# Two mixture-of-experts layers: the rows of the expert weights laid out by neighbours on a partition

## The chip, the cores and the metric

The kernel runs on one core of a Trainium2 chip, as one program. The metric is the device time of an execution in microseconds. The core has five engines that this text names as the profile does: PE (TensorE, products), whose loads of the stationary operand are shown as PEld, DVE (VectorE), ACT (ScalarE), POOL (GpSimd) and SP (SyncE), which issues most of the DMA.

## The reference

It is a block of two layers over 512 tokens of 1024 channels, in float32. The first layer is a convolution and dilated attention, a cross attention over 256 memory rows, and a mixture of experts. The second has a state space branch, a forgetting attention, and a mixture of experts of its own. The change touches the two mixtures only. For each token a router takes the best of 4 groups and in it the best 2 of 8 experts; the expert computes

```python
def expert_block(args):
    xb, e = args
    return (jax.nn.silu(xb @ w1[e]) * (xb @ w3[e])) @ w2[e]
```

and the outputs are summed with the gates of the two experts. The first layer's experts have w1 and w3 of [1024, 512] and w2 of [512, 1024], 6.29 MB each; the second layer's (there w_expert_gate, w_expert_up, w_expert_down) are half as wide, 256, and 3.15 MB. Both have 32.

## The kernel before

**Experts.** Every expert gets 64 slots; two experts make a pair of 128 slots, so there are 16 pairs per layer (`experts`, L1188). Tokens beyond the slots go in further units (`rest`, and for the second layer one unit within the stream). A pair runs through `up`, `down` and `scatter`. `up` (L1075) multiplies xg, the gathered token columns in 8 K chunks of 128 channels, by the up weights; the weights are the moving operand of 512 columns, and each expert's 64 slots are a stationary operand of 64 columns, so the two experts' products run side by side on PE's two halves. An fp32 product is two records in the profile. SiLU and the product of the two branches give hg. `down` (L1093) transposes hg in chunks of 128 (L1098), copies them to hgT, and multiplies by w_down in two halves of 512 output columns (L1110). `scatter` (L1115) multiplies by a one-hot matrix in fp32r (L1125, L1126) and DVE adds to the residual stream X (L1128).

**Gather.** In the first layer `gather` (L1059) makes xg for two pairs at a time by products: the stationary operand is a chunk of 128 channels of the token rows (hh and hl, high and low part, L1066 and L1067), the moving one the one-hot matrix. The gain of the norm is put on per channel while the result is copied out of PSUM. In the second layer the rows come from DRAM by an indirect DMA (`fetch`) and `columns` (L1147) transposes them; `first_columns` makes the first 128 slots by products.

**Weights.** `loads` (L1000) makes the list of loads of a pair: tiles of 1 MB (8 KB on a partition). In the first layer a pair has 12: two halves of the K rows for w1 and for w3 (L1027), and two halves of the output columns for w_down (L1016), of each expert. In the second layer a pair has 6: two K halves, each with gate and up side by side (two DMAs, L1027), and one w_down (L1020), per expert. SyncE issues them in this order into a ring of buffers; before the layer begins 16 or 17 are on their way (`ahead`, `step`). In DRAM a K chunk is 128 rows that follow each other, row p to partition p:

```python
return w[e, rows, cols].rearrange("(c p) n -> p c n", p=128)
```

so what one partition takes in one run is a row, or half of one: 2 KB in the first layer, 1 KB (gate, up) and 4 KB (w_down) in the second.

**Order.** The program is written as a sequence, but the order on each engine is made by the framework's planner, which simulates the program on a timeline of its own (`schedule_with_timeline_sim=True`). So products of the next pair's up stand between those of this pair's scatter.

Of the kernel before, what the change touches and what calls it, by code (L numbers as in the profile page):

```python
# [33 lines left out]
class Halves:  # L34
    """Weight tiles out of a pool of 16 KB tiles."""
# [11 lines left out]
class Slots:  # L47
    """The next 8 KB of a ring of weights; the ring may run over several pools."""
# [10 lines left out]
class K:  # L59
# [58 lines left out]
    def split(self, pool, pieces, eng=None):  # L118
        """float32 [128, kc, n] pieces into high and low parts of 12 bits each, by K chunk."""
# [15 lines left out]
    def load_unit(self, cols, kc=8):  # L135
        """256 columns of a [kc * 128, n] weight (in pieces)"""
        t = self.wt().rearrange("p (c n) -> p c n", c=8)
        o = 0
        for c in cols:
            w = c.shape[1]  # L140
            self.nc.sync.dma_start(t[:, :kc, o:o + w], c.rearrange("(c p) n -> p c n", p=128))
            o += w
        return t[:, :kc, :o]
# [7 lines left out]
    def heads_T(self, wk, tpt, r4, qT, kh, kl, i):  # L151
        """Rows r4 [128, 2 blocks, (2 q, 2 k), 64] transposed, per head: (high; low) of q, (high; high) and
        (low; low) of k on the partitions, so that two products make q k exactly."""
# [18 lines left out]
    def tok_mm(self, act, ws, tiles, nb, n, first=True, last=True, kcs=None):  # L172
        """tiles[b // per] accumulate act^T @ w for token blocks; several blocks share a bank"""
# [10 lines left out]
    def col_mm(self, act, ws, tiles, nt, width, act_c0=0):  # L184
        """tiles accumulate w^T @ act: weight columns on the partitions"""
# [19 lines left out]
    def rsq(self, pool, out, src, scale, eps):  # L205
        """out = (src * scale + eps) ** -0.5 on small tiles, by Newton's iteration."""
# [14 lines left out]
    def raw_T(self, psum, xb, gcol, hi, lo, nb, tag="tp", tpb=2):  # L221
        """x, transposed, times the gain, in two parts"""
# [16 lines left out]
    def norm_T(self, work, psum, xb, gcol, hi, lo, nb, tpb=2):  # L239
        """x (scaled in place by 1/rms), transposed, times the gain, in two parts"""  # L240
# [20 lines left out]
def red2pi(nc, pool, x, shape, name, rounds, shift=0.0):  # L261
    """x (may be modified) -> reduced to [-pi, pi], in place."""
# [18 lines left out]
def load_cols(k, a, rows, ps):  # L281
    """Every per-channel vector as columns: cols[:, i] holds 128 channels."""
# [21 lines left out]
def clamp_sin(nc, pool, out, r, shape, shift, name):  # L304
    """sin(r + shift) for r in about [-pi, pi]."""
# [33 lines left out]
def count_mask(k, wm, lnm, W, row, rep):  # L339
    """8 ln(number of branches that hold the key), or -1e30, as a function of q - k: made once for the  # L340
    1023 distances, then laid out along the diagonals by way of DRAM."""
# [26 lines left out]
def dense1(k, a, Xt, m1, ring1, more, dram, dbg):  # L368
# [7 lines left out]
    # before the residual stream is in it, its tile holds what the first phase needs in float32  # L376
# [7 lines left out]
    with ExitStack() as st:  # L384
# [15 lines left out]
        # ---- norms of x and mem  # L400
        hT = k.pair(k.big_l)
        with ExitStack() as s0:
# [22 lines left out]
            # the rows go in as they are, 1/rms onto the products  # L425
# [11 lines left out]
            # ---- convolution branch, channels on partitions  # L437
# [17 lines left out]
        with ExitStack() as s0:  # L455
# [64 lines left out]
            def after(n, what):  # L520
                """Keep the tensor engine's part of it behind the n-th last product of scores."""
                with tc.issue_after(marks[-n]):
                    what()
# [110 lines left out]
            # 1/rms of the attention output goes onto the product  # L634
# [5 lines left out]
        # ---- output projection, cross attention  # L640
# [39 lines left out]
        def xq(h):  # L680
            # keys and values of the head
# [76 lines left out]
class Moe:  # L758
    """Two-level routing, then every expert over 64 slots of its tokens.

    Tokens beyond that go in units of 128: one of them in the stream of experts where `spare` is set,
    the others in a loop. The norm's 1/rms is not on the gathered rows but on the products.
    Rows are gathered by products with one-hot matrices; or, with `rows`, from a copy in DRAM that holds
    a token's row, its gates and 1/rms."""
# [4 lines left out]
    def __init__(self, k, X, ff, w_a, w_b, w_down, gname, wg, bg, wr, br, spare, rows=None):  # L769
        self.rows = rows  # L770
        self.k, self.X, self.ff, self.spare, self.tag = k, X, ff, spare, gname
        self.w_a, self.w_b, self.w_down = w_a, w_b, w_down
        self.wg, self.bg, self.wr, self.br = wg, bg, wr, br

    def consts(self, pool):
        k, nc = self.k, self.k.nc
        self.gcol = k.gcol(self.tag, 8)
        self.brow = pool.tile([128, 36], F32, name="brow" + self.tag)
# [11 lines left out]
    def snapshot(self, pool):  # L790
        """Where the rows go that the experts gather."""
        self.hh, self.hl = [t.rearrange("p a b -> p (a b)").rearrange("p (b d) -> p b d", b=NB) for t in self.k.pair(pool)]

    def feed(self, wk, tp, pl, u):
        """256 columns of the finished residual stream: rows in two parts, squares, router."""
# [21 lines left out]
    def route(self, keep, wn, st):  # L817
        """Norm, router, ranks: keep gets what the experts need."""
# [22 lines left out]
        def warm(x, n):  # L841
            """keeps the clock of the tensor engine up while it has nothing to do"""
# [12 lines left out]
        def argmax(vals, n, m, name):  # L855
            """the first place of the max over the last axis, as a one-hot row"""
# [11 lines left out]
        # the best two experts of every group, the best group  # L868
# [14 lines left out]
        # e * 64 + 1  # L883
# [13 lines left out]
        # slot + 1, or 0  # L897
# [6 lines left out]
        # the first slots' one-hot matrix  # L904
# [12 lines left out]
    def gates(self, wn, t, gl, gm, gs, m4, As, e1, r, cnt):  # L917
        """What the scatter needs: softmax over the groups, and over the two experts; the units of the
        tokens beyond the slots."""
# [19 lines left out]
        # okey: e * 512 + rank  # L939
# [23 lines left out]
        # how the tokens beyond the slots are cut into units  # L963
# [19 lines left out]
    # ---- experts  # L983
# [6 lines left out]
    def weights(self, es, wt, q=None):  # L990
        """Weights of the experts (indices, or one dynamic slice): K chunks by expert."""
# [8 lines left out]
    def loads(self, es, W, wt, q=None):  # L1000
        """What loads a tile each, in the order of their use."""
# [4 lines left out]
        def src(w, e, rows, cols=slice(None)):  # L1006
            if isinstance(e, int):
                return w[e, rows, cols].rearrange("(c p) n -> p c n", p=128)
            return w[e, rows, cols].rearrange("a (c p) n -> p (a c) n", p=128)

        def load_down(dst, e, h):
            """w_down, by halves of its columns"""
            t = wt()
            if self.ff == 512:
                t = t.rearrange("p (c n) -> p c n", c=4)
                q.dma_start(t, src(self.w_down, e, slice(0, 512), slice(h * 512, h * 512 + 512)))  # L1016
                dst[4 * h:4 * h + 4] = [t[:, j] for j in range(4)]
            else:
                t = t.rearrange("p (c n) -> p c n", c=2)
                q.dma_start(t, src(self.w_down, e, slice(0, 256)))  # L1020
                dst[:] = [t[:, j, i * 512:i * 512 + 512] for i in range(2) for j in range(2)]

        def load(ws, dst, e, h, c=4):
            t = wt().rearrange("p (c n) -> p c n", c=c)
            n = t.shape[2] // len(ws)
            for i, w in enumerate(ws):
                q.dma_start(t[:, :, i * n:i * n + n], src(w, e, slice(h * c * 128, (h + 1) * c * 128)))  # L1027
            dst[h * c:h * c + c] = [t[:, j] for j in range(c)]
# [11 lines left out]
    def ahead(self, wt, n, order=()):  # L1040
        """n tiles may be under way before their use, in this order of their use's places."""
# [11 lines left out]
    def pair(self, p):  # L1053
        """Weights of a pair, all of its loads emitted."""
        while any(x is None for part in self.early[p] for e in part for x in e):
            self.todo.pop(0)()
        return self.early[p]

    def gather(self, wk, ps, sel, n, first=False):  # L1059
        nc = self.k.nc  # L1060
        xg = wk.tile([128, KC, 256], F32, name="xg", bufs=1)
        for c in range(KC):
            p = (self.idle_bank(ps, c) if first else ps.tile([128, 512], F32, name="g"))[:, :n]
            for b in range(NB):
                cs = slice(c * 128, (c + 1) * 128)
                nc.tensor.matmul(p, self.hh[:, b, cs], sel[:, b, :n], start=b == 0, stop=False)  # L1066
                nc.tensor.matmul(p, self.hl[:, b, cs], sel[:, b, :n], start=False, stop=b == NB - 1)  # L1067
            g = self.gcol[:, c:c + 1]
# [6 lines left out]
    def up(self, wk, ps, xg, W, parts, r, own=None):  # L1075
        """parts: (expert of W, slot range in xg, partition range out)"""
# [16 lines left out]
    def down(self, wk, ps, hg, W, parts):  # L1093
# [3 lines left out]
        for j in range(nt):  # L1097
            nc.tensor.transpose(pt[:, j * 128:(j + 1) * 128], hg[:, j * 128:(j + 1) * 128], k.ident)  # L1098
# [1059 lines left out]
```

## Time and profile before

| What | Value |
| --- | --- |
| Median of 3 runs | 1862.99 us (1860.67 to 1866.47) |
| Span of the profiled execution | 1851.7 us |
| Its own device time | not on the page; the median is 11.3 us above the span |
| PE busy | 1742.1 us, 94% of the span |
| DVE, ACT, POOL busy | 945.8, 557.4, 326.2 us |
| Granted PE clock, mean | 0.982 |
| DMA | 397.61 MB, mean 215 GB/s |

The span reaches from the first to the last instruction of one execution. A share of busy time is an average over stages; the first layer's experts run from about 508 to 1085 us, the second layer's from about 1530 us to the end. Starts and lengths of PE's instructions overlap, since products are pipelined; what a product costs is seen from the distance of the starts.

### The profile page before, as it was taken

How to read it: one execution, taken by the hardware profiler on the slowest of the kernel's cores; microseconds unless marked ns; L12 is line 12 of the kernel's file. 1: busy time of each engine (PE TensorE's matmuls, PEld its weight loads, DVE VectorE, ACT ScalarE, POOL GpSimd, SP SyncE). 2: the span in 40 equal slices, each digit the busy share in tenths (PEclk: the TensorE clock that was granted, in tenths of full speed). 3: DMA queues.
4: the chain of work that ended last, by engine and by line, in shares of the span. 5: the costliest groups of instructions: out<-in, count | busy, mean ns of one | idle time of the engine just before them, and what ended most of it. 6: DMA issues, size and time to landing. Idle time of an engine off the chain costs nothing. (4 is left out here: it accounts for less than half of the span.)

```text
span 1851.7 us, 26034 instructions
## 1 busy us (share of the span) xinstructions
PE 1742.1 (94%) x10153; PEld 1163.3 (63%) x10153; DVE 945.8 (51%) x2104; ACT 557.4 (30%) x1192; POOL 326.2 (18%) x435
## 2 busy tenths in 40 slices
PE   7999999999899999999999987999999999999998
PEld 5999999989744444434343345788997883334433
DVE  8984566554626333343333357714664554464454
ACT  5365666443212111000001033333656322112111
POOL 2211121112202210311123013201222401010000
PEclk9999999999899999999999998989999999999999
DMA  6322232326588999999899872624441957999991
GB/s 186 98 80 62 76 115 85 108 70 228 132 286 305 389 355 333 377 345 351 316 347 349 311 203 35 106 66 91 69 69 43 333 171 242 369 371 369 370 330 47
DMA packets 265873, 397.61 MB, mean 215 GB/s; under 512 B 15003, under 2 KB 147282, under 8 KB 265745
## 3 DMA queue, kind: packets, MB, share of 16 engines
q1 hardware_dynamic: 248648, 369.15, 60.5%
q0 software_dynamic: 5680, 16.75, 3.1%
q10 hardware_dynamic: 11416, 9.99, 1.8%
q8 instruction: 82, 1.34, 0.3%
q14 instruction: 47, 0.38, 0.1%
HBM read 386.87 MB, written 9.51 MB: 214 GB/s over the span
## 5 line engine op out<-in xcount | busy, mean ns | idle before, releaser
L1128 DVE TENSOR_TENSOR X<-X,y 128x512 f32<-128x512 f32 x264 | 173.6, 684 | 216.0 <-PE y L1126 215.2
L114 PE MATMUL mm<-wh,b 128*128 128x256 f32 x832 | 235.0, 285 | 3.1 <-DVE rb L510 1.6
L115 PE MATMUL mm<-wl,b 128*128 128x256 f32 x832 | 235.7, 284 | 2.3 <-POOL wl L128 2.1
L116 PE MATMUL mm<-wh,b 128*128 128x256 f32 x832 | 233.8, 284 | 0.0
L1086 PE MATMUL h<-w,xg 128*64 128x512 f32 x712 | 200.7, 599 | 0.0
L128 POOL TENSOR_TENSOR wl<-w,wh 128x1024 fp32r<-128x1024 f32 x38 | 92.8, 2443 | 496.6 <-ACT wh L125 430.3
L125 ACT ACTIVATE wh<-w 128x1024 fp32r<-128x1024 f32 x112 | 118.4, 1058 | 144.5 <-PE mm L115 68.6
L115 PEld LDWEIGHTS mm<-wl,b 128*128 128x128 f32 x832 | 158.4, 190 | 4.2 <-POOL wl L128 2.5
L114 PEld LDWEIGHTS mm<-wh,b 128*128 128x128 f32 x832 | 157.7, 190 | 5.0 <-issue 1.9
L116 PEld LDWEIGHTS mm<-wh,b 128*128 128x128 f32 x832 | 157.9, 191 | 0.5
L1120 ACT ACTIVATE oh<-o,gate 128x512 fp32r<-128x512 f32 x64 | 44.0, 688 | 317.0 <-PE o L1110 243.5
L114 PE MATMUL mm<-b,wh 128*128 128x512 f32 x320 | 125.3, 404 | 5.6 <-ACT wh L125 2.5
L115 PE MATMUL mm<-b,wh 128*128 128x512 f32 x320 | 128.0, 400 | 1.3 <-DVE b L203 1.3
L116 PE MATMUL mm<-b,wl 128*128 128x512 f32 x320 | 125.5, 397 | 0.3 <-DVE wl L128 0.3
L1125 PE MATMUL y<-oh,sT 128*128 128x512 f32 x256 | 115.2, 463 | 11.2 <-DVE X L1128 7.9
L1110 PE MATMUL o<-w,hgT 128*64 128x512 f32 (+1 forms) x384 | 117.0, 609 | 6.7 <-DVE hgT L1102 5.8
L128 DVE TENSOR_TENSOR wl<-w,wh 128x1024 fp32r<-128x1024 f32 x74 | 95.0, 1284 | 46.0 <-ACT wh L125 45.6
L1110 PE MATMUL o<-b,hgT 128*64 128x512 f32 x392 | 113.9, 608 | 3.7 <-DVE hgT L1102 3.2
L1125 PEld LDWEIGHTS y<-oh,sT 128*128 128x128 f32 x256 | 46.4, 187 | 111.6 <-issue 45.7
L1086 PEld LDWEIGHTS h<-w,xg 128*64 128x64 f32 x712 | 56.7, 136 | 89.3 <-issue 85.5
L1086 PE MATMUL h<-b,xg 128*64 128x512 f32 x312 | 101.6, 601 | 0.0
L1126 PE MATMUL y<-ol,sT 128*128 128x512 f32 x256 | 98.4, 398 | 0.4 <-DVE ol L1121 0.2
(679 smaller groups left out, 3244.2 us busy)
## 6 DMA issues: line engine op xcount, KB each, us to landing
w<-in_w_dram SPq DMA_DIRECT2D x124, 1024.0 KB, 10.2
b<-in_w_dram SPq DMA_DIRECT2D x68, 1024.0 KB, 9.6
b<-in_w_expert_down_dram SPq DMA_DIRECT2D x20, 1024.0 KB, 10.1
w<-in_w_expert_gate_dram SPq DMA_DIRECT2D x36, 512.0 KB, 9.7
w<-in_w_expert_up_dram SPq DMA_DIRECT2D x36, 512.0 KB, 9.0
w<-in_w_in_dram SPq DMA_DIRECT2D x17, 1024.0 KB, 11.5
b<-in_w_expert_gate_dram SPq DMA_DIRECT2D x30, 512.0 KB, 10.1
b<-in_w_expert_up_dram SPq DMA_DIRECT2D x30, 512.0 KB, 10.2
```

Of the source, the lines that this page charges most:

```text
L114: nc.tensor.matmul(out, sh, mh, start=start, stop=False, skip_group_check=True)
L115: nc.tensor.matmul(out, sh, ml, start=False, stop=False, skip_group_check=True)
L116: nc.tensor.matmul(out, sl, mh, start=False, stop=stop, skip_group_check=True)
L125: nc.scalar.activation(hi[:, :kc, :n], src, AF.Copy)
L128: e.tensor_sub(lo[:, :kc, :n], src, f(hi[:, :kc, :n]))
L1086: nc.tensor.matmul(h[po], xg[:, c, ss], fw[e][c], start=c == 0, stop=c == KC - 1, skip_group_check=True)
L1110: nc.tensor.matmul(o[po], hT[:, j, po], W[2][e][half * nt + j], start=j == 0, stop=j == nt - 1, skip_group_check=True)
L1120: self.k.last = nc.scalar.activation(oh, outs[half], AF.Copy, scale=gate)
L1125: nc.tensor.matmul(y, sT[:, bs], oh, start=True, stop=False)
L1126: nc.tensor.matmul(y, sT[:, bs], ol, start=False, stop=True)
L1128: nc.vector.tensor_add(xs, xs, y)
```

## The change

A run of neighbouring rows goes to one partition: with c rows per partition, partition p takes rows p*c to p*c + c - 1, which lie side by side in DRAM. For w1 and w3 c is 4 (of each half of the K rows), so a run has 8 KB in the first layer and 4 KB in the second. K chunk c of a half then holds every fourth channel, and xg must have its channels in the same order: the gather, `columns` and `first_columns` take their stationary operand with a step of 4 elements (`chan`), and the gains are loaded again in that order (`gain`, one more small DMA per layer on GpSimd's queue). w_down is cut by rows in both layers, 256 rows to a tile with c = 2, runs of 8 KB; the transposes of hg take every second column. In the first layer a tile of w_down now serves both halves of the outputs for two of four K chunks. The second layer's up weights lie as all of gate's chunks and then all of up's, so the moving operand of a product is two runs of 256. The calls in `whole` pass the gain vectors on. Comments of the file are taken out too.

```diff
 class Moe:
-    def __init__(self, k, X, ff, w_a, w_b, w_down, gname, wg, bg, wr, br, spare, rows=None):
+    def __init__(self, k, X, ff, w_a, w_b, w_down, gname, gain, wg, bg, wr, br, spare, rows=None):
...
+        self.g = gain
...
     def consts(self, pool):
...
+        self.gain = pool.tile([128, 2, 4], F32, name="gain" + self.tag)
+        nc.gpsimd.dma_start(self.gain, self.g.rearrange("(h p c) -> p h c", h=2, c=4))
+        self.gain = self.gain.rearrange("p h c -> p (h c)")
...
     def loads(self, es, W, wt, q=None):
...
-        def src(w, e, rows, cols=slice(None)):
+        def src(w, e, rows):
             if isinstance(e, int):
-                return w[e, rows, cols].rearrange("(c p) n -> p c n", p=128)
-            return w[e, rows, cols].rearrange("a (c p) n -> p (a c) n", p=128)
+                return w[e, rows].rearrange("(p c) n -> p c n", p=128)
+            return w[e, rows].rearrange("a (p c) n -> p (a c) n", p=128)
 
         def load_down(dst, e, h):
-            t = wt()
-            if self.ff == 512:
-                t = t.rearrange("p (c n) -> p c n", c=4)
-                q.dma_start(t, src(self.w_down, e, slice(0, 512), slice(h * 512, h * 512 + 512)))
-                dst[4 * h:4 * h + 4] = [t[:, j] for j in range(4)]
-            else:
-                t = t.rearrange("p (c n) -> p c n", c=2)
-                q.dma_start(t, src(self.w_down, e, slice(0, 256)))
-                dst[:] = [t[:, j, i * 512:i * 512 + 512] for i in range(2) for j in range(2)]
+            t = wt().rearrange("p (c n) -> p c n", c=2)
+            q.dma_start(t, src(self.w_down, e, slice(h * 256, h * 256 + 256)))
+            nt = self.ff // 128
+            for i in range(2):
+                for j in range(2):
+                    dst[i * nt + 2 * h + j] = t[:, j, i * 512:i * 512 + 512]
 
         def load(ws, dst, e, h, c=4):
-            t = wt().rearrange("p (c n) -> p c n", c=c)
-            n = t.shape[2] // len(ws)
+            t = wt().rearrange("p (i c n) -> p i c n", i=len(ws), c=c)
             for i, w in enumerate(ws):
-                q.dma_start(t[:, :, i * n:i * n + n], src(w, e, slice(h * c * 128, (h + 1) * c * 128)))
-            dst[h * c:h * c + c] = [t[:, j] for j in range(c)]
+                q.dma_start(t[:, i], src(w, e, slice(h * c * 128, (h + 1) * c * 128)))
+            dst[h * c:h * c + c] = [t[:, 0, j] if len(ws) == 1 else t[:, :, j] for j in range(c)]
...
+    @staticmethod
+    def chan(c):
+        return slice(c // 4 * 512 + c % 4, c // 4 * 512 + 512, 4)
...
     def gather(self, wk, ps, sel, n, first=False):
...
-                cs = slice(c * 128, (c + 1) * 128)
+                cs = self.chan(c)
                 nc.tensor.matmul(p, self.hh[:, b, cs], sel[:, b, :n], start=b == 0, stop=False)
                 nc.tensor.matmul(p, self.hl[:, b, cs], sel[:, b, :n], start=False, stop=b == NB - 1)
-            g = self.gcol[:, c:c + 1]
+            g = self.gain[:, c:c + 1]
...
     def down(self, wk, ps, hg, W, parts):
...
-            nc.tensor.transpose(pt[:, j * 128:(j + 1) * 128], hg[:, j * 128:(j + 1) * 128], k.ident)
+            cs = slice(j // 2 * 256 + j % 2, j // 2 * 256 + 256, 2)
+            nc.tensor.transpose(pt[:, j * 128:(j + 1) * 128], hg[:, cs], k.ident)
...
     def columns(self, wk, ps, xr):
...
-                o = (4 * h + c) * 128
-                nc.tensor.transpose(p[:, c], xr[:, o:o + 128], self.k.ident)
+                nc.tensor.transpose(p[:, c], xr[:, self.chan(4 * h + c)], self.k.ident)
...
     def first_columns(self, wk, ps):
...
-                nc.tensor.matmul(p, self.X[:, b, c * 128:(c + 1) * 128], sel[:, b], start=b == 0, stop=b == NB - 1)
-            nc.scalar.activation(xg[:, c], p, AF.Copy, scale=self.gcol[:, c:c + 1])
+                nc.tensor.matmul(p, self.X[:, b, self.chan(c)], sel[:, b], start=b == 0, stop=b == NB - 1)
+            nc.scalar.activation(xg[:, c], p, AF.Copy, scale=self.gain[:, c:c + 1])
```

## Rows read from the trace of the kernel before

**Rows 1.** The page: busy share of DMA in 40 slices, in tenths.

```profile
DMA  6322232326588999999899872624441957999991
```

**Rows 2.** Windows: us; busy by engine (count); then PEclk, DMA share, GB/s.

```profile
560.00:1060.00 500.00, 477.37 (x2181) 208.49 (x2179) 190.90 (x443) 48.63 (x84) 104.77 (x177) 0.99 0.95 344
1575.00:1800.00 225.00, 221.49 (x894) 89.00 (x890) 116.88 (x210) 41.05 (x98) 17.44 (x44) 1.00 1.06 365
```

**Rows 3.** Waits of PE, 560 to 1060 us: total us, times, longest.

```profile
PE pt L1098 <- DVE hg L1090: 9.3, 10, 0.9
PE o L1110 <- DVE hgT L1102: 8.2, 7, 2.7
```

**Rows 4.** PE's weight loads by form: busy us, mean ns | idle <-releasers.

```profile
L1086 PEld LDWEIGHTS h<-w,xg 128*64 128x64 f32 x536 | 43.1, 136 | 66.1 <-issue 62.7 <-DMA w<-in_w_dram 1.4 <-DMA b<-in_w_dram 0.3
L1086 PEld LDWEIGHTS h<-b,xg 128*64 128x64 f32 x300 | 25.8, 136 | 42.3 <-issue 40.3 <-DMA w<-in_w_dram 0.4
L1086 PEld LDWEIGHTS h<-b,xgr 128*64 128x64 f32 x170 | 13.0, 136 | 22.5 <-issue 20.4 <-ACT xgr L1160 1.0 <-DMA w<-in_w_expert_up_dram 0.7
```

**Rows 5.** Waits of SyncE's queue, 560 to 1060 us.

```profile
SPq L1027 <- PE h L1086: 156.6, 47, 13.3
```

**Rows 6.** Timeline of PE, second layer: start, length, instructions.

```profile
1662.51 0.66 PE L1155 MATMUL g<-ident,xr 128*128 128x128 f32 x4
...
1664.11 0.50 PE L1125 MATMUL y<-oh,sT 128*128 128x512 f32 x1
...
1664.68 0.39 PE L1125 MATMUL y<-oh,sT 128*128 128x512 f32 x1
1664.91 0.40 PE L1126 MATMUL y<-ol,sT 128*128 128x512 f32 x1
1665.23 0.64 PE L1086 MATMUL h<-b,xgr 128*64 128x512 f32 x1
...
1665.71 0.59 PE L1086 MATMUL h<-b,xgr 128*64 128x512 f32 x1
...
1668.29 0.59 PE L1086 MATMUL h<-b,xgr 128*64 128x512 f32 x1
...
1668.82 0.66 PE L1155 MATMUL g<-ident,xr 128*128 128x128 f32 x4
```

**Rows 7.** The same at the end of the kernel.

```profile
1836.22 3.65 PE L1110 MATMUL o<-b,hgT 128*64 128x512 f32 x16 [0.53 <-ACT hgT L1104]
```

**Rows 8.** DMA, 1660 to 1700 us: rate per us; timeline of SyncE.

```profile
GB/s 401 409 398 366 356 349 350 348 347 348 349 378 394 366 349 351 371 397 398 418 406 383 374 351 346 349 351 368 388 416 373 350 351 355 398 373 364 347 349 347
...
1670.84 2.91 SPq L1020 DMA_DIRECT2D b<-in_w_expert_down_dram  x2
```

**Rows 9.** DMA, 780 to 820 us: rate per us.

```profile
GB/s 387 389 385 391 383 387 389 385 391 381 387 389 385 391 385 385 381 365 121 317 401 387 410 389 160 0 63 258 397 404 406 389 307 344 348 397 403 393 174 319
```

**Rows 10.** Timeline of SyncE, first layer; time to landing at L1016.

```profile
781.86 15.74 SPq L1016 DMA_DIRECT2D w<-in_w_dram  x4
...
DMA to landing us min/median/max: 5.1/8.8/11.9
```

**Rows 11.** Timeline of PE: the reader of these loads.

```profile
817.75 1.07 PE L1110 MATMUL o<-w,hgT 128*64 128x512 f32 x2 [0.78 <-DVE hgT L1102]
```

**Rows 12.** Line L1066: its loads, ns min/median/max.

```profile
L1066 PEld LDWEIGHTS g<-sel,b x232: 185/188/193, 500.4 to 1025.6; 128*128 128x128 f32 x116
```

**Rows 13.** Line L1641: its loads, and four products in the timeline.

```profile
L1641 PEld LDWEIGHTS tp<-ident,s x32: 131/133/153, 1147.0 to 1170.3; 128*64 128x64 f32 x32
...
1147.18 0.60 PE L1641 MATMUL tp<-ident,s 128*64 128x128 f32 x4
```

**Rows 14.** Timeline of PE: eight gather products, first and last.

```profile
1025.05 0.28 PE L1066 MATMUL g<-sel,b 128*128 128x256 f32 x1
...
1025.87 0.28 PE L1067 MATMUL g<-sel,b 128*128 128x256 f32 x1
```

**Rows 15.** Line L783: issue on GpSimd, ns.

```profile
L783 POOL DMA_DIRECT2D wrtnorm_ffn_g<-in_w_router_expert_dram x1: 889/889/889, 483.1 to 483.1; - x1
```

More of the change, by code (lines that the diff above doesn't have):

```diff
@@ L1153, in columns @@
             for c in range(4):
-                o = (4 * h + c) * 128
-                nc.tensor.transpose(p[:, c], xr[:, o:o + 128], self.k.ident)
+                nc.tensor.transpose(p[:, c], xr[:, self.chan(4 * h + c)], self.k.ident)
             if h:
-                nc.vector.tensor_tensor(xg[:, 4:8], p, self.gcol[:, 4:8, None].to_broadcast([128, 4, 128]), op=OP.mult)
+                nc.vector.tensor_tensor(xg[:, 4:8], p, self.gain[:, 4:8, None].to_broadcast([128, 4, 128]), op=OP.mult)
             else:
                 for c in range(4):
-                    nc.scalar.activation(xg[:, c], p[:, c], AF.Copy, scale=self.gcol[:, c:c + 1])
+                    nc.scalar.activation(xg[:, c], p[:, c], AF.Copy, scale=self.gain[:, c:c + 1])
         return xg
@@ L2070, in whole @@
     dram = k.pool("dr", space=DRAM)
-    m1 = Moe(k, X, 512, a["w1"][0], a["w3"][0], a["w2"][0], "moe_norm_g", a["w_group"][0], a["b_group"][0],
+    m1 = Moe(k, X, 512, a["w1"][0], a["w3"][0], a["w2"][0], "moe_norm_g", a["moe_norm_g"][0], a["w_group"][0], a["b_group"][0],
              a["w_router"][0], a["b_router"][0], spare=False)
     m2 = Moe(k, X, 256, a["w_expert_gate_2"][0], a["w_expert_up_2"][0], a["w_expert_down_2"][0], "norm_ffn_g_2",
-             a["w_router_group_2"][0], a["b_router_group_2"][0], a["w_router_expert_2"][0], a["b_router_expert_2"][0], spare=True,
+             a["norm_ffn_g_2"][0], a["w_router_group_2"][0], a["b_router_group_2"][0], a["w_router_expert_2"][0], a["b_router_expert_2"][0], spare=True,
              rows=dram.tile([S, D + 33], F32, name="xrow"))
```

## The prediction

> **What bounds the kernel now.** I read the page first, its forty slices above all [rows 1]. The DMA line stands at 8 or 9 in slices 12 to 23 (the first layer's experts, 32 of width 512) and at 9 in 35 to 39 (the second layer's, 32 of width 256). Only these two stretches load what the change rearranges, so the question is what they wait for.
>
> The windows by stage [rows 2] take the long part of each, 500 and 225 us. In them PE is busy for 477.37 of 500 us and for 221.49 of 225 us, at a granted clock of 0.99 and 1.00. DMA is busy too, at a share of 0.95 and 1.06, so the share of busy time does not tell which one rules. The releasers do. PE's idle time in these windows [rows 3] ends with DVE or ACT work: 9.3 us at the transposes of hg, 8.2 us at the first product of w_down; no DMA is named. A weight load of PE can carry the wait instead of the product, so I read those rows too [rows 4]: four waits for weights on their way, 1.4 + 0.3 + 0.4 + 0.7 = 2.8 us in 725 us, and these are idle times of the loading side, hidden behind the product before. On the other side SyncE, which issues the loads, waits for PE to give buffers back [rows 5]: 156.6 us in the first window for up products alone. Weights wait for PE, not PE for weights.
>
> That PE also runs at its own pace, not at a pace set by arriving tiles, is seen in the timeline [rows 6]: within a run of up products the starts follow each other by 0.43 us (1665.71 to 1668.29, six steps of alike record pairs), and at the end, when all loads have landed, 16 records of the down product take 3.65 us, or 0.43 us for each concurrent pair and a tail [rows 7]. The stream is the same whether DMA is saturated or idle.
>
> **The change part by part.**
>
> *Longer runs in DRAM.* The transfers do get faster. In the second layer the rate goes up and down with what is in flight [rows 8]: 347 to 351 GB/s under gate and up (1 KB runs), and a peak of 418 some 8 us after two loads of w_down have been issued (4 KB runs, SyncE at 1670.84). In the first layer, with runs of 2 KB, the full slices stand at 381 to 391 [rows 9]. I take 406, the slice beside that peak, for all that is 4 KB and longer: the first layer moves 32 x 6.29 = 201.3 MB, 201.3/0.388 = 519 us against 201.3/0.406 = 496 us, 23 us less; in the second layer gate and up are 67.1 MB, 192 us against 165 us, 27 us less; w_down there goes from 4 to 8 KB, which no row prices, and I leave it. So 50 us of queue time are saved. What hides them is PE's own work, 477 of 500 and 221 of 225 us; DMA was under that cover before and is further under it after. What can come back is the 2.8 us above at the most, since beyond it nobody waits for weights. I take 1 us, and 0 to 2.8 as its bounds.
>
> *w_down by rows.* In the first layer the first half of the outputs now needs both tiles of an expert. The second tile (rows 256 to 511) is first read after two K chunks and not after four: 4 record pairs of 0.43 us, 1.7 us earlier; the first tile is given back as much later. The lead covers that: four loads issued from 781.86 to 797.6 us, landing after 8.8 us in the median and 11.9 at worst [rows 10], so by 810 at the latest, and their first reader starts at 817.75 [rows 11]. Cost 0; if the lead were gone it would be 1.7 us for each of 16 pairs, 27 us.
>
> *Stationary operands with a step.* Channels of a chunk are now 4 elements (16 bytes) apart, for 512 loads of the gather (8 groups x 8 chunks x 4 blocks from hh, as many from hl; 232 of one kind are in one row) [rows 12], for the 128 of `columns` (16 x 8), and for the 32 of `first_columns`; transposes of hg step by 2. No row has a 128-column load with a step of 16 bytes. The nearest is L1641 in the state space part, which takes every eighth element (32 bytes): 64 columns in 133 ns, four products in 0.60 us [rows 13], against 136 ns for 64 adjacent columns of an ordinary product at L1086 [rows 4]. So a wide step cost no more per column than an ordinary product's load pays anyway. I take 0 for all of them. The upper bound is a doubled streaming part: 128 adjacent columns take 188 ns and 64 take 136, so 52 ns per 64 columns, 104 ns for 128; doubled, 208 ns would have to pass between gather products that now start every 0.117 us (1025.05 to 1025.87, seven steps) [rows 14]. That is 91 ns x 512 = 47 us, all on PE's path. The transposes have less at stake: 160 x 0.1 = 16 us at the very most.
>
> The Trainium skill has a rule that speaks against this step: "SBUF — State Buffer", section "Door 1: The DMA port swizzle", says that SBUF lines are 16 bytes, that full bandwidth wants two hits in a line, and that each element from a new line pays. By that rule every column of the gather's loads is a new line, and the result is the second rival's, 1909 us and not 1862; the L1641 rows, each element from a new line too, do not bear it out, though they are transposes and half as wide.
>
> *The moving operand of the second layer's up product* is now two runs of 256 (gate, up) and not one of 512. No row has such a pattern; two separate products of 256 take 2 x 0.117 = 0.234 us where one of 512 takes 0.23 (1664.68 to 1664.91) [rows 6, 14], so even a full restart at the seam costs some 4 ns, at 2 x 264 records 2 us at most. I take 0.
>
> *The gain columns.* Two DMAs more on GpSimd's queue, 0.9 us each by the neighbours of the same routine [rows 15], at 6 us and at 482 us, ahead of the first layer's experts. Behind them in its queue stand other small loads that nobody on PE's path waits for at that time. Cost 0, bound 1.8 us. The gather's scale comes from the new columns with unchanged instructions.
>
> *The sum.* -1 (weights) + 0 + 0 + 0 + 0 on a span of 1851.7 us. The page gives no device time of its own execution; the median of the runs is 1862.99 us, 11.3 us more than this span, and I leave that difference as it is. Forecast: **1862 us**.
>
> **The rivals.**
>
> *First, the order gets tighter: faster.* The order on PE is laid out by a planner with its own picture of when tiles arrive, and the stream is cut accordingly: the up products are left at 1662.51, 1664.11 and 1668.82 us, for transposes or the scatter [rows 6]. Each interruption costs: the last fp32 pair is followed after 0.53 us and not 0.43 (1668.29 to 1668.82), the way back takes 0.32 us and not 0.23 (1664.91 to 1665.23, against 1664.68 to 1664.91), and the first pair 0.48 (1665.23 to 1665.71), together 0.24 us. At one in 3.2 us the 225 us hold some 70 of them, 17 us, by estimate from these rows; the first layer has the same kind. If earlier tiles let the planner join half of those in the second layer, and some in the first, 11 us go: 1851 us. For it: the runs come in pieces that no data dependence of the products themselves asks for. Against: nothing in the diff asks for another order.
>
> *Second, strided loads slow the gather: slower.* The place is L1066 and L1067; it decides from the point where streaming 128 columns takes longer than the 117 ns between products, 13 ns above what it takes now. With doubled streaming 47 us: 1909 us. Against: L1641.
>
> *Third, the order gets looser: slower.* The same price as in the first, the other way: w_down's first half, held for a second tile, is laid out later, and the runs are cut once more. +11 us: 1873 us. The idle rows at the transposes of hg and the first down product (17.5 us in the first layer) show where a shifted order would hurt at once.
>
> *Fourth, the change does what it says and PE was waiting after all.* Then up to the 3.5 us that PE is not busy in the second window, and little of the first's 22.6, could return: 1859 us, hardly outside no change. I count it into the forecast.
>
> **How the numbers follow.** A measurement of this kernel can tell about 0.3%, 5.6 us, from no change. Forecast 0.52, tighter order 0.20, strided gather 0.14, looser order 0.14. Of the forecast's 0.52, 0.02 end faster and 0.03 slower than 0.3% by the unpriced ends. Faster 0.20 + 0.02 = 0.22; slower 0.14 + 0.14 + 0.03 = 0.31; same 0.47. The forecast's own range is 1857 to 1868. The range that should hold the time 8 times in 10 takes in both orders with their ends, 1848 to 1884, and leaves out the full price of the strided gather.
>
> **What would show each step right or wrong.** Right: the slices of GB/s in the second layer near 406 throughout, SyncE waiting longer for PE, PE's busy time in both windows as before, weight loads of L1066 and L1067 still at 188 ns and starting every 0.117 us, hg's waits at 9 and 8 us. Wrong: loads at L1066 or L1067 well above 188 ns with products further apart than 0.117 us (second rival); the same instructions with the same durations, but other counts of interruptions or other waits at L1098 and L1110 (first and third); PE waiting for `w` or `b` by a DMA (w_down's lead gone).

## The result and the profile after

The changed kernel is slower: 1920.95 us in the median of 4 runs (1918.54 to 1923.27) beside 1862.45 us for the kernel before on the same chip, a ratio of 1.0312, with a 95% interval of 1.0296 to 1.0328. That is 58.5 us more. The profiled execution has a span of 1918.6 us, 66.9 us above that of before; the profiled execution of before was one of its quickest (its later executions lasted 1851.82 to 1868.42 us), and those 8 us come from there. (The device time of an execution is not 11 us above its span: for the profiled one of after it is 1920.37 us beside 1918.6.)

First the transfers, where the change does what it says. The page of after, DMA in 40 slices (before: [rows 1]):

```profile
DMA  5321242225586986969788774443440845999881
```

Windows of after (us; busy by engine and count; PEclk, DMA share, GB/s), a stretch of each layer as long as those in [rows 2]:

```profile
600.00:1100.00 500.00, 483.70 (x1985) 238.72 (x1985) 163.38 (x330) 42.46 (x70) 99.02 (x158) 0.99 0.80 315
1600.00:1825.00 225.00, 222.27 (x908) 90.98 (x904) 109.52 (x218) 43.21 (x103) 21.24 (x52) 1.00 0.91 354
```

The DMA share falls from 0.95 to 0.80 and from 1.06 to 0.91, while PE is busy for even more of its time: 483.70 of 500 us. The transfers are quicker, and nobody was waiting for them. SyncE now waits longer for PE to give buffers back (156.6 us for up products in [rows 5]). Waits of SyncE, 600 to 1100 us (total, times, longest):

```profile
SPq L1028 <- PE h L1092: 201.7, 54, 16.1
SPq L1028 <- PE o L1117: 100.9, 12, 12.8
```

and PE's own waits in that stretch [rows 3] are shorter than before, all on DVE or ACT:

```profile
PE o L1117 <- DVE hgT L1109: 7.3, 6, 2.6
PE pt L1105 <- DVE hg L1096: 6.7, 7, 1.2
```

So the time is not in a wait. It is in PE's own instructions. The stationary loads of after by line (count: ns min/median/max, first and last start), where [rows 12] had 185/188/193; L1072 is the gather, L1182 `first_columns`, L1161 `columns`, L1105 the transposes of hg:

```profile
L1072 PEld LDWEIGHTS g<-sel,b x232: 307/330/334, 499.2 to 1088.1; 128*128 128x128 f32 x116
...
L1182 PEld LDWEIGHTS y<-ssrow,X x24: 329/329/329, 1585.3 to 1596.3; 128*128 128x128 f32 x24
...
L1161 PEld LDWEIGHTS g<-ident,xr x120: 195/210/222, 1607.7 to 1892.6; 128*128 128x128 f32 x120
...
L1105 PEld LDWEIGHTS pt<-ident,hg x98: 194/208/219, 536.9 to 1902.3; 128*128 128x128 f32 x98
```

The last three of these in the kernel before, in the same order:

```profile
L1176 PEld LDWEIGHTS y<-ssrow,X x24: 191/192/193, 1524.8 to 1530.7; 128*128 128x128 f32 x24
...
L1155 PEld LDWEIGHTS g<-ident,xr x120: 137/140/144, 1541.1 to 1825.7; 128*128 128x128 f32 x120
...
L1098 PEld LDWEIGHTS pt<-ident,hg x98: 137/141/146, 531.0 to 1835.3; 128*128 128x128 f32 x98
```

And the timeline of gather products, which stood 0.117 us apart in [rows 14] (start, length):

```profile
1061.86 0.40 PE L1073 MATMUL g<-sel,b 128*128 128x256 f32 x1
1062.09 0.40 PE L1072 MATMUL g<-sel,b 128*128 128x256 f32 x1
...
1063.26 0.40 PE L1073 MATMUL g<-sel,b 128*128 128x256 f32 x1
```

Six steps in 1.40 us, 0.233 us each: the next product waits for its load. To see what each kind of instruction is worth, I summed over the trace the distance from the start of each PE record to the start of the next:

| PE records | count | before, us | after, us | difference |
| --- | --- | --- | --- | --- |
| gather | 512 | 69.0 | 127.1 | +58.1 |
| first_columns | 64 | 8.1 | 15.1 | +7.0 |
| columns | 128 | 17.3 | 18.5 | +1.2 |
| transposes of hg | 98 | 23.5 | 25.2 | +1.6 |
| up | 1552 | 399.4 | 403.2 | +3.8 |
| down and scatter | 1303 | 370.4 | 365.8 | -4.5 |

The six differences, taken before rounding, make 67.2 us, and the spans differ by 66.9 us. Nearly all of it is where the stationary operand of a product has a step of four elements.

### The profile page after: what moved, and what is told of

Its sections match the earlier page's. It is cut to its first block, busy times and chain, and to the rows that moved or that the text cites. A ratio compares the mean times of both kernels' runs of the same rounds, so it can differ in the third digit from the quotient of the medians.

```text
span 1918.6 us, 26038 instructions
## 1 busy us (share of the span) xinstructions
PE 1820.6 (95%) x10153; PEld 1244.0 (65%) x10153; DVE 944.5 (49%) x2104; ACT 558.4 (29%) x1192; POOL 332.5 (17%) x437
## 5 line engine op out<-in xcount | busy, mean ns | idle before, releaser
L128 POOL TENSOR_TENSOR wl<-w,wh 128x1024 fp32r<-128x1024 f32 x38 | 96.9, 2550 | 502.2 <-ACT wh L125 464.6
```

Source lines behind the costliest of these rows:

```text
L128: e.tensor_sub(lo[:, :kc, :n], src, f(hi[:, :kc, :n]))
```

## The experiments

The theory to test: a product's stationary load whose columns lie in different 16-byte pieces of SBUF is slower, and the gather goes at the pace of its loads. The rivals: the faster transfers disturb PE's reads; or the order of the work, or w_down by rows, is what costs.

**Everything of the change, but adjacent loads in the gather.** ACT and GpSimd, which write hh and hl, put the four channels of a partition's run apart, so that the gather reads 128 adjacent ones:

```diff
-            nc.scalar.activation(self.hh[:, :, cs], X[:, :, cs], AF.Copy)
-            nc.gpsimd.tensor_sub(self.hl[:, :, cs], X[:, :, cs], f(self.hh[:, :, cs]))
+            x = X[:, :, cs].rearrange("p b (q c) -> p b q c", c=4)
+            hh, hl = [t[:, :, u // 2 * 512:u // 2 * 512 + 512].rearrange("p b (c q) -> p b q c", c=4)[:, :, u % 2 * 64:u % 2 * 64 + 64] for t in (self.hh, self.hl)]
+            nc.scalar.activation(hh, x, AF.Copy)
+            nc.gpsimd.tensor_sub(hl, x, f(hh))
...
-                cs = self.chan(c)
+                cs = slice(c * 128, (c + 1) * 128)
```

> The changed kernel, but the rows that the gather reads (hh, hl) are stored with the channels of a chunk side by side, so that the 512 stationary loads of the gather take adjacent elements again; the weights keep their long runs. Theory (the step in the stationary operand is the cost): loads of the gather back from about 327 to 188 ns, its products back from 0.233 to 0.117 us apart, 58 us gone, so 1863 us; with what is left of the step at first_columns (7 us), columns (1) and the transposes of hg (2) the range is 1860 to 1872 us. Rival (the faster transfers write into SBUF while PE reads it, and slow its loads): the loads stay above 300 ns and the time within 1915 to 1925 us. Second rival (the order on PE or w_down by rows is the cost): loads at 188 ns but a time well above 1880 us.

Measured: 1860.09 us beside 1858.49, ratio 1.0011 (0.9994 to 1.0027). Its loads, the gather and `first_columns`, which still has its step:

```profile
L1074 PEld LDWEIGHTS g<-sel,b x232: 186/188/201, 501.4 to 1030.2; 128*128 128x128 f32 x116
...
L1184 PEld LDWEIGHTS y<-ssrow,X x24: 329/329/329, 1527.2 to 1538.2; 128*128 128x128 f32 x24
```

With the long runs in place and the transfers as quick as in after (336 GB/s in 600 to 1100 us, 315 in after), the loads are back at 188 ns and the loss is gone. The transfers are cleared. Writing with a step, on engines that are off the path, shows no cost. (The 10 us that were left for the other steps don't show in full; the runs below find what offsets them.)

**The step alone, in the old layout.** The reverse: the kernel before, short runs and w_down by columns, with hh and hl stored so that each load takes every fourth element.

```diff
...
-                cs = slice(c * 128, (c + 1) * 128)
+                cs = slice(c // 4 * 512 + c % 4, c // 4 * 512 + 512, 4)
```

> The kernel before, with its short runs and w_down by columns, but the rows of the gather stored so that each stationary load takes every fourth element (16 bytes apart); the values gathered are the same. Theory (step): loads 325 to 330 ns, products 0.233 us apart, 512 x 0.116 = 59 us more than before, 1918 to 1924 us. Rivals (faster transfers, or the order): 1860 to 1870 us, loads at 188 ns.

Measured: 1920.37 us, ratio 1.0353 (1.032 to 1.0386). The gather's start distances sum to 127.2 us, as in after; the order of PE's expert work is that of before, record for record.

```profile
L1068 PEld LDWEIGHTS g<-sel,b x232: 307/330/334, 499.5 to 1086.7; 128*128 128x128 f32 x116
```

The step alone brings the whole loss, without a longer run anywhere.

**Steps of two and of eight.** The same edit with other numbers.

> As the run with every fourth element, but every second (8 bytes apart). If what costs is a new 16-byte line for each element, two elements share a line here and the loads stay near 188 ns: 1860 to 1866 us. If any step but one costs the same, the loads are at 325 to 330 ns and the time is 1918 to 1924 us. If the cost grows with the step, something between.

> As the run with every fourth element, but every eighth (32 bytes apart). By both the line theory and the theory that any step costs: loads at 325 to 330 ns and 1918 to 1924 us. If the cost grows with the bytes between elements: loads above 400 ns and a time above 1950 us.

Measured: 1865.97 us for every second element, 1927.25 us for every eighth (one execution each). The loads of the two kernels:

```profile
L1068 PEld LDWEIGHTS g<-sel,b x232: 192/195/200, 499.0 to 1029.5; 128*128 128x128 f32 x116
```

```profile
L1068 PEld LDWEIGHTS g<-sel,b x232: 312/338/346, 501.0 to 1094.3; 128*128 128x128 f32 x116
```

The products stand 121 ns apart at a step of two, 234 at four, 241 at eight. So for these loads two elements in 16 bytes are nearly as good as four, one is not, and beyond that the distance hardly matters. That is the rule of the Trainium skill ("SBUF — State Buffer", section "Door 1: The DMA port swizzle") which the prediction set against its row: 16-byte lines, two hits wanted in each. For the loads of products the traces agree with it: 188 and 195 ns with four and two hits, 330 with one. These four steps can't tell a line of 16 bytes from a mere distance between 8 and 16 bytes, and the loads of transposes already pay at a step of two (below). The price is 142 ns per load, of which 117 come through to the pace of the products.

**The row that misled.** The prediction took the cost of a step from L1641 [rows 13]. Here its 32 transposes read adjacent columns.

```diff
-                                        uT[:, 2 * h + c].rearrange("p (c i) -> p i c", i=8)[:, 2 * i2 + i], k.ident)
+                                        uT[:, 2 * h + c, (2 * i2 + i) * 64:(2 * i2 + i) * 64 + 64], k.ident)
```

> The kernel before, but the 32 transposes of line 1641 take 64 adjacent columns and not every eighth element, which leaves the channels of the state space branch in the wrong order; nothing else differs. Theory (the row of line 1641 from which the step was priced at nothing already held the price of a step, because an adjacent transposing load of 64 columns is shorter than a product's): its loads 95 to 105 ns and not 133, worked out from 140 ns for 128 adjacent transposing columns and 206 to 208 ns for 128 with a step. Rival (a step costs a transpose of 64 columns nothing): 131 to 135 ns as before. The time stays within 0.3% of before in either case.

```profile
L1641 PEld LDWEIGHTS tp<-ident,s x32: 108/111/113, 1144.9 to 1168.2; 128*64 128x64 f32 x32
```

111 ns and not 133 (and not the 95 to 105 I expected). The row did hold the price of a step, 22 ns on 64 columns; it was hidden because the load of a transpose is shorter than that of a product with as many columns (136 ns) to begin with. The time, 1859.34 us in one execution, did not move.

**Runs of two rows.** The change with runs of two rows, so a step of two everywhere:

```diff
...
-        return slice(c // 4 * 512 + c % 4, c // 4 * 512 + 512, 4)
+        return slice(c // 2 * 256 + c % 2, c // 2 * 256 + 256, 2)
...
-            for i, w in enumerate(ws):
-                q.dma_start(t[:, i], src(w, e, slice(h * c * 128, (h + 1) * c * 128)))
+            for i, w in enumerate(ws):
+                for o in range(2):
+                    q.dma_start(t[:, o, i], src(w, e, slice(h * c * 128 + o * 256, h * c * 128 + o * 256 + 256)))
...
```

> The changed kernel with runs of two neighbouring rows and not four: channels of a chunk 2 elements (8 bytes) apart, in both layers, the rows of the gather stored in plain order as in the changed kernel; w_down by rows as there. Theory (a load of an ordinary product pays for each 16-byte line, and two elements share one here): gather loads 188 to 198 ns, its products 0.117 to 0.121 us apart (2 us more than before), first_columns about 0.113 us apart (not 0.233), transposes in columns 0.120 and not 0.109 us apart (1.4 us), hg the same (1.6 us): 1859 to 1864 us, 1.000 to 1.003 of before. Rival (the plain-order run with a step of 2 was cheap for another reason, the short runs): 1900 us or more.

Measured: 1871.24 us beside 1860.14, ratio 1.0072 (1.0047 to 1.0097), above what the theory gave. The loads of the gather, of `columns` and of `first_columns`:

```profile
L1073 PEld LDWEIGHTS g<-sel,b x232: 192/195/255, 500.2 to 1035.0; 128*128 128x128 f32 x116
...
L1162 PEld LDWEIGHTS g<-ident,xr x120: 194/207/231, 1547.1 to 1837.6; 128*128 128x128 f32 x120
...
L1183 PEld LDWEIGHTS y<-ssrow,X x24: 194/196/197, 1530.2 to 1537.6; 128*128 128x128 f32 x24
```

The loads came out as expected: 195 and 196 ns, products 120 and 118 ns apart. What is new is the order. This layout needs twice as many transfers for the up weights, and the planner laid PE's expert work out otherwise: its records (gather, `first_columns`, `columns`, transposes of hg, up, down, scatter) fall into 565 uninterrupted stretches of one kind and not 513, and it goes from up to down or back 64 times and not 33. Up products take 411.7 us of start distances and not 399.4, 9.0 of the 12.3 us more in the second layer, where the median distance is 422 ns in both kernels; down takes 208.9 and not 204.1, the scatter 160.8 and not 166.3. That is the prediction's third rival, the looser order, in a kernel in which it was not expected, and at about its price (+13 us against +11). That the number of transfers brings the other order was not tried.

**The first layer alone.** Adjacent gather loads, long runs and w_down by rows in the first layer, the second layer as before:

```diff
...
+            pc = "(p c)" if self.ff == 512 else "(c p)"
...
-        return slice(c // 4 * 512 + c % 4, c // 4 * 512 + 512, 4)
+        return slice(c * 128, (c + 1) * 128)
...
```

> The first layer as in the run with adjacent rows (long runs, w_down by rows, hh and hl stored so that the gather's loads are adjacent), the second layer as in the kernel before, so no step at first_columns and columns. Theory (what the adjacent-rows run still paid was the step at first_columns, 7.0 us, and at columns, 1.2 us): 8 us less than that run, so 1850 to 1854 us, 0.995 to 0.998 of the kernel before. Rival (that run's rest came from the order, and the first layer's long runs give nothing): 1858 to 1862 us, within 0.2% of before. If the second layer's longer runs were worth something, this run loses it and is slower than 1862 us.

Measured: 1853.72 us beside 1860.14, ratio 0.9966 (0.9952 to 0.998). That is 0.45%, 8.4 us, below the adjacent-rows kernel, where 7.0 + 1.2 us for the second layer's steps were expected. Without any step of four a part of the change must be worth 0.3%. Which?

**w_down by rows alone**, and the kernel before once more as a null comparison:

```diff
...
-                q.dma_start(t, src(self.w_down, e, slice(0, 512), slice(h * 512, h * 512 + 512)))
-                dst[4 * h:4 * h + 4] = [t[:, j] for j in range(4)]
...
+            rows = self.w_down[e, h * 256:h * 256 + 256]
+            q.dma_start(t, rows.rearrange("(p c) n -> p c n", p=128) if isinstance(e, int) else rows.rearrange("a (p c) n -> p (a c) n", p=128))
...
+            for i in range(2):
+                for j in range(2):
+                    dst[i * nt + 2 * h + j] = t[:, j, i * 512:i * 512 + 512]
...
```

> The kernel before with one part of the change: w_down by rows, in both layers, and with it the transposes of hg by every second element; the other weights and the gather as before. Theory (the second tile's lead covers the 1.7 us by which it is needed earlier): transposes of hg 0.120 and not 0.109 us apart, 1.6 us in all, 0.998 to 1.003 of before. Rival (the lead is gone, or the order is cut more): 10 to 27 us more, 1868 to 1886 us, with waits of down's loads for DMA.

> The kernel before itself, once more, as a measure of what a comparison can tell: ratio 0.998 to 1.002 with an interval that holds 1. If it comes out at 0.995 to 0.997 like the three runs with small edits (first layer only, w_down by rows, short runs), their 0.4% is what any kernel shows here and none of it belongs to the edits.

> The same kernel as w_down by rows alone, once more beside that null comparison. If its gain is real: 0.995 to 0.998, below the null comparison, with 3 to 4 us less in the first layer's down and scatter products. If not: as the null comparison.

Measured: 0.9964 (0.9948 to 0.998) the first time and 0.9951 (0.9936 to 0.9965) the second, in which the null comparison gave 0.9998 (0.9978 to 1.0018). The gain is real, 7 to 9 us, and more than was expected. Groups of PE's instructions for the kernel before, from its second profile (span 1856.7 us; 600 to 1100 us; count, busy, mean ns, idle before and what ended it):

```profile
L1125 PE MATMUL y<-oh,sT 128*128 128x512 f32 x112 | 48.3, 456 | 5.7 <-DVE X L1128 2.7 <-ACT oh L1120 2.6
...
L1098 PE MATMUL pt<-ident,hg 128*128 128x128 f32 x52 | 8.4, 284 | 9.5 <-DVE hg L1090 8.3 <-DVEq L1344 1.2
```

and with w_down by rows, again from the second profile:

```profile
L1124 PE MATMUL y<-oh,sT 128*128 128x512 f32 x112 | 48.1, 449 | 3.1 <-DVE X L1127 2.9
...
L1097 PE MATMUL pt<-ident,hg 128*128 128x128 f32 x52 | 9.5, 305 | 7.6 <-DVE hg L1088 6.4 <-DVEq L1343 1.2
```

The wait of the scatter for ACT (2.6 us) is gone. The timelines of the same two profiles show why, first before, then by rows:

```profile
819.78 3.65 PE L1110 MATMUL o<-w,hgT 128*64 128x512 f32 x16
824.26 0.73 PE L1125 MATMUL y<-oh,sT 128*128 128x512 f32 x2 [0.83 <-ACT oh L1120]
825.05 0.74 PE L1126 MATMUL y<-ol,sT 128*128 128x512 f32 x2
825.71 3.65 PE L1110 MATMUL o<-w,hgT 128*64 128x512 f32 x14
```

```profile
825.85 1.93 PE L1109 MATMUL o<-w,hgT 128*64 128x512 f32 x4 [0.78 <-DVE hgT L1101]
...
828.27 7.08 PE L1109 MATMUL o<-w,hgT 128*64 128x512 f32 x28
835.28 0.73 PE L1124 MATMUL y<-oh,sT 128*128 128x512 f32 x2
```

Before, the scatter of the first half of the outputs cuts into the down products of the second, and PE stands for 0.83 us until ACT has scaled the first half. By rows the planner runs both halves through, and the scaling is done meanwhile.

The start distances of gather, up, transposes, down and scatter in the first layer sum to 564.2 and 564.1 us in the two profiles by rows, and to 566.8 and 570.7 us in the two of the kernel before. The order is thus worth some 2.6 us; the two profiles of before have the same order, and what parts them is mostly the granted clock under the down products, which take 138.2 and 141.7 us: behind two waits of the scatter, 0.83 us for ACT and 0.54 for DVE, the second profile has 0.50 in 979 to 980 us, the lower level, and there the pairs of down products stand 0.85 us apart; in the first the like waits, 0.83 and 0.55 us, pass at 1.00. The executions say the same: by rows the mean granted clock is 0.982 and 0.981 in the median of the two rounds, before 0.978, and where both had 0.981 by rows took 1853.5 us in the mean of 6 executions and before 1855.7 in the mean of 6. So of the 7 to 9 us some 2 to 3 come at an equal clock, and the rest goes with a higher clock. By rows the wait for ACT before such a fall is gone, but that this is what raises the clock is not shown.

The expert work of PE has the same order, record for record, in this kernel, in after, in the adjacent-rows and in the first-layer kernel (506 stretches); so all of them have the order's gain, and after hides it under its loss. Why the planner chose so was not tried.

**Shorter runs.** The kernel before with the first layer's weights in runs of 1 KB:

```diff
...
-                q.dma_start(t[:, :, i * n:i * n + n], src(w, e, slice(h * c * 128, (h + 1) * c * 128)))
+                for o in range(0, n, 256):
+                    q.dma_start(t[:, :, i * n + o:i * n + o + 256], src(w, e, slice(h * c * 128, (h + 1) * c * 128), slice(o, o + 256)))
```

> The kernel before with the first layer's weights in runs of 1 KB and not 2 KB (two transfers for each tile): 201.3 MB at 349 and not 388 GB/s, 577 and not 519 us of transfer time. Theory (transfers are covered by PE's work, and only what exceeds it shows): 0 to 30 us more than before, with waits of w loads for DMA in the first layer; loads of PE unchanged at 188 and 136 ns. Rival (the first layer runs at the rate of its transfers): 58 us more, 1916 us.

Measured: 1852.28 us beside 1860.14, ratio 0.9959 (0.9939 to 0.998): not slower, even 0.4% quicker. The page's rates in 40 slices, and the largest of SyncE's waits for PE in 600 to 1100 us, where [rows 5] had 156.6 in a like stretch:

```profile
GB/s 185 97 80 62 76 114 88 106 70 225 132 281 310 352 351 351 355 350 351 346 350 336 335 186 37 99 70 91 69 69 27 347 170 227 368 372 369 369 337 46
```

```profile
SPq L1029 <- PE h L1088: 25.7, 18, 3.5
```

The first layer now moves its weights at 346 to 355 GB/s in eight slices without a pause (14 to 21), the rate of 1 KB runs in [rows 8], and SyncE has almost no slack left; still nobody waits for a weight longer than 0.4 us. That is the cover of the prediction, tested: it holds even where the transfers take some 58 us more (201.3 MB at 349 and not 388 GB/s). The 0.4% stays open. The order on PE is another here too (510 stretches), but no run ties the gain to it; the clock does not account for it, since at 0.979 three of its executions took 1853.3 us in the mean, and ten of before 1859.3.

## Why the prediction was wrong

*Longer runs: right.* DMA shares fall, SyncE waits longer for PE, and in the kernel with long runs and adjacent loads the time is that of before (1.0011). The sign that I had named, 406 GB/s throughout the second layer, was a poor one: the rate of after there is 354 in the mean, and SyncE waits 64.1 us for up products and 44.6 for down products in 1600 to 1825 us: transfers that are hidden run no faster than PE gives buffers back.

*w_down by rows: right in that the lead holds, wrong in the sum.* No down product waits for its weights; but the term is not 0: by rows alone is 7 to 9 us quicker, some 2 to 3 of them by the order on PE at an equal clock, the rest with a higher granted clock. This is the first rival, the tighter order (priced at 11 us), and it came together with the second, which the list of rivals, one case at a time, did not allow for. "Nothing in the diff asks for another order" was the wrong reason: with w_down cut by rows, and nothing else, the planner made another order.

*Stationary operands with a step: the step that failed.* I took 0 for all of them, because 133 ns at L1641 looked like the 136 ns of an adjacent load. The two loads are of different kinds, a transpose and a product. Beside an adjacent transpose the row shows +22 ns, and a product pays far more than a transpose: 142 ns for 128 columns against 67 to 70 (hg 141 to 208, columns 140 to 210 ns), and the transposes hide most of that (109 and 110 ns apart before, 121 and 120 after). The upper bound failed as well: doubled streaming gave 91 ns for each of 512 products and 47 us; it was 117 ns and 58.1 us. And `first_columns`, named but not priced, brought 7.0 us; its 32 products are 64 loads in the trace. With these the second rival's sum is 58.1 + 7.0 + 1.2 for the steps, and -0.4%, some 8 us, for w_down by rows with its transposes and its clock: +58 us, which is what was measured. The range ended at 1884 because it left out that rival's full price.

*The moving operand in two runs, and the gain columns: right.* Up products that follow each other in the second layer stand 422 ns apart in the median (421 before), and their start distances sum to 134.1 us (135.5 before). All that PE does outside the experts sums to 954.7 us (955.1 before), so the two small DMAs for the gains cost nothing there.

## What to carry to other kernels

Before a layout is changed for the sake of transfers, look whether anybody waits for them; here kernels with the first layer's runs at 1, 2 and 8 KB and no step of four in it came out within 0.4% of each other. A layout with neighbouring rows on a partition puts a step into the operand on the other side: keep two elements of a product's load within 16 bytes, or let an engine that is off the path write with the step, so that PE's loads stay adjacent. And price an instruction by a row of its own kind, transpose by transpose and product by product, since the difference between kinds can hide just what one is looking for.

## What the runs showed of the hardware

- An fp32 stationary load of 128 columns for a product takes 188, 195, 330 and 338 ns at steps of 1, 2, 4 and 8 elements. The load of a transpose takes 140 ns adjacent and already 207 at a step of two (hg and the two-row kernel's columns), 210 at four. That the two kinds of load begin to pay at different steps I had not expected, and no run here says why.
- Executions of the kernel before last from 1852 to 1868 us, and the time goes with the mean granted clock of the execution: 1852.82 us at 0.982, 1861.54 at 0.979, 1867.81 at 0.972. All lie near the higher of the two levels, 2.4 GHz; the lowest stretch in the profile of before is 1100 to 1200 us, between the two layers, 0.91 with PE busy for 85.99 of 100 us. The same products at the same place can get another clock in another execution: behind the like waits of PE, 0.5 to 0.8 us each, 1.00 in one profile of before and 0.50 in the other (979 to 980 us).
- A difference of some tenths of a per cent can come from an edit of the weights' layout through the order that the planner makes of it, and through the clock that goes with it: -0.4% (w_down by rows) and +0.7% (two-row runs) here, with as many products of the same shapes.
- No kernel of these runs is shown to be quicker than w_down by rows alone, 0.9951 and 0.9964 of before, with nothing else of the change; the first layer alone (0.9966) and the shorter runs (0.9959) cannot be told from it.
